# Expert steps of 1024 inner columns instead of 512

## The chip, the cores and the metric

The kernel runs on one core of a Trainium2 chip. The metric is the device time of one execution in microseconds (us). Before the change it was 2018.52 us, the median of three runs (2017.03, 2019.66 and 2018.52).

A core has a matrix engine (PE, with its weight loads listed apart as PEld), a vector engine (DVE), a scalar engine (ACT), a general engine (POOL) and an engine that here only issues DMAs (SP). Each runs its own instruction stream in order; semaphores join them. PE writes into eight banks of PSUM (each 128 x 512 float32), and ACT and DVE read them from there into SBUF.

## The reference

The reference is a backbone of two layers over 256 latent tokens with a context prefix of 256 tokens, 1024 wide: a mixer of three kinds of attention heads and then a feed-forward block, each with a norm, a modulation and a gated residual. The feed-forward block of the first layer is dense. That of the second takes about half of the time, and the change touches it alone: a router picks two of eight experts for each latent token, and each expert is a SwiGLU with 3584 inner columns.

```python
def swiglu(h, w_gate, w_up, w_down):
    return (jax.nn.silu(h @ w_gate) * (h @ w_up)) @ w_down

def moe_swiglu(h, w_router, w_gate, w_up, w_down):
    logits = (h @ w_router).astype(jnp.float32)
    top_v, top_i = lax.top_k(logits, TOP_K)          # 2 of 8
    top_w = jax.nn.softmax(top_v, axis=-1)
    combine = ...                                    # weight of each expert for each token, mostly 0
    out = jnp.zeros_like(h)
    for e in range(N_EXPERTS):                       # w_gate[e], w_up[e]: 1024 x 3584, w_down[e]: 3584 x 1024
        out = out + combine[..., e:e + 1] * swiglu(h, w_gate[e], w_up[e], w_down[e])
    return out
```

Everything is float32. The three matrices of an expert are 14 MB each, 336 MB for the eight, and all of it is read.

## The kernel before

**Arithmetic.** A product of float32 matrices is done as three PE matmuls on parts: each operand is split exactly into a high and a low part (w = h + l, both of a type that PE multiplies fast), and h·h, l·h and h·l are added up in one PSUM bank (`mm3`, lines 289 to 291). A weight arrives by DMA as a raw tile of 1 MB. Each piece of half a tile (128 x 1024 elements) is then split: ACT casts the high part (line 150), DVE subtracts it from the raw tile for the low part (line 151). Both write one buffer `whl`, of which there are four, so the split runs up to four pieces ahead of PE. The helper `split` (lines 295 and 296) does the same for activations: a cast on ACT, then a subtraction on DVE.

**The ring of raw tiles.** SP issues the loads in the order of use (line 138) into a ring of 8 + `NRAWM` = 13 raw tiles; a load waits until DVE has subtracted the tile that was in its buffer.

**An expert.** The tokens of an expert sit in 128 slots, as two transposed parts `xh` and `xl`. The 3584 inner columns are worked through in 7 steps of 512. A step s has these parts, in the order in which the main loop (lines 1644 to 1672) emits them:

- `turn(s)`: PE transposes the activations of step s by four 128 x 128 transposes into one bank `pt` (line 1518), ACT copies `gh` from it (line 295), DVE subtracts `gl` (line 296).
- `gate_up(s + 1)` for the gate and then for up: 8 chunks of rows, 3 matmuls of 512 columns each, into one bank `pg` and one bank `pu` (lines 1496 and following, matmuls on lines 289 to 291).
- `activate(s + 1)`: ACT takes the silu of `pg`, DVE multiplies by `pu`, into a buffer `sg` (lines 1510 and 1511).
- `down(s)`: 4 chunks of the 512 inner columns by the two halves of the 1024 output columns, 24 matmuls that add into two banks `pd`, which are held through all steps of an expert.

So PE turns the results of a step only after the down products of the step before it, and there is always the gate and up of one step between a turn and the down products that use it.

**The small work between the matmuls.** After every piece of weights the function `tick` counts, and at every third tick it emits one closure from a queue: the result of the expert before (`weigh`, `high` and `low`: `yt` on DVE, line 1566, `yh` on ACT, line 1569, `yl` on DVE, line 1572), its scatter back to the tokens (a pair of matmuls into a bank `psc`, lines 1580 and 1581, and an addition to `xl` on DVE, line 1585), the gathering of the tokens for the next pair of experts (8 matmuls into a bank `pgt`, line 1468, `gtmp` on ACT or DVE, then a split into `xh` and `xl`) and the transposed one-hot rows (bank `pw`). What hasn't been emitted in time is emitted by `flush` ahead of the next expert's gate products or ahead of the first down products.

**Buffers.** Banks of PSUM come from two groups of four. Group b holds `pg` and `pu`. Group c holds the two `pd`, and everything else (`pt`, `pgt`, `psc`, `pw`) shares its other two. Buffers go round in order of request, and a new use of a buffer waits until the last reader of the old one is done. `sg`, `gh`, `gl`, `yt`, `yh`, `yl` and `gtmp` share `NT2M` = 6 SBUF buffers of 128 x 512 in the same way.

**Order.** In this stage PE, ACT and DVE keep the order in which the program is written: an instruction that waits holds up all that is behind it on its engine.

Of the kernel before, what the change touches and what calls it, by code (L numbers as in the profile page):

```python
# [29 lines left out]
NSTEP = DFE // 512  # L30
GRID_W = 64

# columns of the table of constants
# [10 lines left out]
NRAWM, NSPLITM, NT2M, NXG = 5, 4, 6, 2  # L44
# [3 lines left out]
BR = 4  # L48
# [20 lines left out]
def _constants():  # L69
    """Identity, triangles, selectors and the rotary tables: they depend on the shapes alone."""  # L70
# [35 lines left out]
def reverse(t):  # L106
    """[p, n] read from the last column to the first."""
    (ps, p), (_, n) = t.ap
    return bass.AP(tensor=t.tensor, offset=t.offset + n - 1, ap=[[ps, p], [-1, n]])
# [6 lines left out]
class Weights:  # L116
    """The weights in the order in which they are used: loads run ahead in a ring, and each float32 tile is
    split exactly into two float32r parts (w = h + l), in one or two pieces, shortly before its products."""
# [54 lines left out]
    def take(self, key, j=0):  # L173
        """The next piece: its two parts, or itself where it isn't split; as [128, nk, n]."""
        i, p, _, _ = self.pieces[self.ntake]
        assert self.plan[i][0] == key and p == j, (self.plan[i][0], p, key, j)
        self.pump()
        self.ntake += 1
        return self.hl[self.ntake - 1] if self.plan[i][2] else self.raw[i]
# [12 lines left out]
def rows_of(w, r0, nk, c0, n):  # L192
    """nk chunks of 128 rows from r0, columns c0..c0+n, as [128, nk, n]."""
    return w[r0:r0 + nk * 128, c0:c0 + n].rearrange("(k p) f -> p k f", p=128)
# [40 lines left out]
def down_tiles(s):  # L235
    """Tiles of the weights of a step: first chunk of 128 rows, chunks, first column, columns. In the last step one half of
    the columns after the other, so that most of what follows goes on beside it."""
    if s < NE * NSTEP - 1:
        return [(0, 2, 0, D), (2, 2, 0, D)]
    return [(r, 2, c, 512) for c in (0, 512) for r in (0, 2)]  # L240


def moe_plan(I):
    plan = []

    def gu(m, s):
        e, n = divmod(s, NSTEP)
        for h in range(2):
            plan.append(((m, s, h), rows_of(I[m][0, e], 512 * h, 4, 512 * n, 512), True))

    S = NE * NSTEP
    for s in range(S + 1):
# [3 lines left out]
        if s > 0:  # L256
            e, n = divmod(s - 1, NSTEP)
            for h, (r, nk, c, cols) in enumerate(down_tiles(s - 1)):
                plan.append((("moe_down", s - 1, h), rows_of(I["moe_down"][0, e], 512 * n + 128 * r, nk, c, cols), True))
# [8 lines left out]
# the blocks of 512 columns of the modulations in the order in which they are worked out  # L268
# [8 lines left out]
def kernel(ctx: ExitStack, tc: tile.TileContext, I, out: bass.AP):  # L277
# [15 lines left out]
    def split(h, l, x):  # L293
        """h + l = x, both float32r."""
# [106 lines left out]
    # silu of the two conditions, the norms' weights and the biases of the modulations, as columns  # L401
# [21 lines left out]
    def mod_block(l, n):  # L423
        """512 columns of the modulation of both streams."""
# [39 lines left out]
    def gate_rows(l, which, streams, new=lambda: t2("grow")):  # L464
        """The gate of the residual, the same in every row: per stream two tiles of 512 columns."""
# [12 lines left out]
    def rstd(b):  # L478
        """1 / rms of the tokens of a block."""
# [12 lines left out]
    def norm_T(l, which, steps, hT):  # L492
        """Into hT, by steps of (stream, chunks of 128 columns in pairs). The product with diag(1 / rms) turns and scales a block."""
# [34 lines left out]
    def ordered(engines):  # L528
        """A region in which these engines keep to the program's order."""
        return tc.manual_schedule(engines={getattr(mybir.EngineType, e) for e in engines})  # L530

    def drain(gen):
        """Run a generator to its end; its value."""
# [10 lines left out]
    def merge(one, two):  # L544
        """Steps of both in turn to the end of `one`; its value."""
# [16 lines left out]
    def alternate(one, two, n):  # L562
        """n steps of `one`, a step of `two`, and so on to the end of both."""
# [11 lines left out]
    def weave(main, fill, every=1):  # L575
        """Emit both, one step of `fill` after every `every` steps of `main`; their values."""
# [18 lines left out]
    def take_in(l, name, hT, step):  # L595
        """The products of a projection by its tiles of weights: step(k, tile's parts, flags)."""
# [10 lines left out]
    def proj_T(l, name, hT, outs):  # L607
        """Columns in the partitions: outs of (bank, its rows, first column, tokens)."""
# [7 lines left out]
    def proj_nat(l, name, hT, nb=4, late=False, group="c"):  # L616
        """Tokens in the partitions, 256 columns: two blocks of 128 tokens in a bank."""
# [8 lines left out]
        if late:  # L626
            # the context first: the latent tokens are ready after it
# [16 lines left out]
    def inputs_gla(l, hT, A):  # L644
# [17 lines left out]
        for r in range(2):  # L662
            # 2 silu(z) = (tanh(z / 2) + 1) z: tanh lies in one table with exp
# [5 lines left out]
    def gla(l, A, mix):  # L669
# [4 lines left out]
        # sums of the log decays (times 16) along each chunk, forward or backward  # L674
# [10 lines left out]
        for d in range(2):  # L685
# [31 lines left out]
            # the states: what each chunk adds, then the walk over the chunks  # L717
# [52 lines left out]
    def head_norm(po, n):  # L770
        """1 / rms over the 64 rows of each head, spread over these rows: po two of [2 heads x 64, n]; [128, n] each."""
# [22 lines left out]
    # rotary tables with the norms' weights and the scale of the scores  # L794
# [30 lines left out]
    def rotate(dst, src, nh, d, cos, sin):  # L825
        """dst = src * cos + swapped halves of src * sin: [128, 2 blocks, nh heads * d], the tables per block."""
# [15 lines left out]
    def head_rstd(src, nh):  # L842
        """1 / rms of nh heads of 64 in two blocks."""
# [10 lines left out]
    def gqa_heads(l, b2, j, src, nh):  # L854
        """Norm and rotary of nh heads of 64 in two blocks (j: 0 q, 1 k)."""
# [12 lines left out]
    def diff_maps(b2, src, scale, t):  # L868
        """Rotary of the 8 maps of 32 in two blocks, times scale."""
# [10 lines left out]
    def stack(t3, kind):  # L880
        """The parts h and l of heads [128, n, d] side by side, for products that contract over 128 rows and hold
        every product of parts: per head h|l (q of GQA), h|h l|l (its k), h|h|l|l (q of a map), h|l|h|l (their k)."""
# [9 lines left out]
    def turned(o, dst):  # L892
        """Transposed into dst [128, 4, 128 tokens]."""
# [7 lines left out]
    def evac(dst, src):  # L901
        """A bank to SBUF, by turns on two engines."""
# [3 lines left out]
    def inputs_diff(l, hT, A, norm):  # L906
        """The operands of the differential heads; in the first layer by the first half of the columns of x while the
        modulations of the others arrive."""
# [56 lines left out]
    def inputs_gqa(l, hT, A):  # L965
        """Keys and values of GQA, then its queries: the four heads of a key head."""
# [27 lines left out]
    def attention(l, A, mix, fill, rate):  # L994
        """Units of four score tiles each (a block of queries, and four maps or heads), as a pipeline: the queries of a
        unit, the scores of the one before and the products with V of the one before that; `fill` between them."""
# [5 lines left out]
        def place(u, g):  # L1002
            """Tile and columns of a score tile: with 256 keys two of them share a tile."""
# [40 lines left out]
        def weigh(u):  # L1044
            """Exponentials into weights: of GQA times 1 / sum, of the two maps their difference."""
# [89 lines left out]
        def at(j, f):  # L1135
            """f of the unit j, as steps."""
# [45 lines left out]
    def products(order, parts, weights, step, nb, end):  # L1182
        """All blocks of tokens by each chunk in turn; by the last two block after block, so that the first are done early."""
# [18 lines left out]
    def order_of(nb):  # L1202
        """Blocks of tokens, the context first."""
        return (2, 3, 0, 1) if nb == 4 else (0, 1)

    def advance(norm, b):
        """Steps of the next norm of the context before the residuals of the latent tokens."""
# [50 lines left out]
    def early():  # L1258
        """The first weights of the experts, as soon as those of the modulations have been used."""
# [33 lines left out]
    def ffn(norm, hT, norm2):  # L1293
        drain(alternate(norm, mods(MODS["ffn"]), EVN[0]))
        act = []
        for j in range(6):
# [6 lines left out]
            for m in ("ffn_gate", "ffn_up"):  # L1303
# [3 lines left out]
                if m == "ffn_gate" and j == 0:  # L1307
                    # the context first: the latent tokens are ready after it
# [73 lines left out]
    def spread(b):  # L1382
        """x / rms in two parts."""
# [5 lines left out]
    # the two largest logits, the lower expert first where they are equal, and their softmax  # L1389
# [7 lines left out]
    # the gate of the residual, while the logits are compared  # L1397
# [12 lines left out]
    # slot of a token with an expert, from 1: how many tokens up to it have chosen it; 0 where it hasn't  # L1410
# [9 lines left out]
    def rest_of_route():  # L1420
        """What isn't needed for the first products: the weights of the experts and the largest number of their tokens."""
# [14 lines left out]
    def experts(W, off):  # L1436
        """Slots off..off+128 of every expert."""
# [18 lines left out]
        def gather(p, d2):  # L1456
            """Columns 256 * d2 .. of the tokens of experts 2p and 2p + 1, modulated, as steps: the products, the parts of
            the first, and later those of the second."""
# [37 lines left out]
        def gate_up(s, m, store):  # L1496
            e = s // NSTEP
            p = store[s] = bank("p" + m[4], "b")
            h_, l_ = XG[e]
            for q in range(4):  # L1500
                wh, wl = W.take((m, s, q // 2), q % 2)
                for kk in range(2):
                    k = 2 * q + kk
                    mm3(p, (h_[:, k], l_[:, k]), (wh[:, kk], wl[:, kk]), start=k == 0, stop=k == KC - 1)
# [3 lines left out]
        def activate(s):  # L1508
            g = t2("sg")
            S.activation(g, ps_g.pop(s), AF.Silu)  # L1510
            V.tensor_tensor(g, g, ps_u.pop(s), op=ALU.mult)
            act[s] = g
# [225 lines left out]
```

## Time and profile before

| what | before |
|---|---|
| median of three runs | 2018.52 us |
| profiled execution: its span, the only time that the page gives for it | 2016.9 us |
| PE busy | 1930.0 us (96%) |
| DVE busy | 1408.0 us (70%) |
| ACT busy | 1182.3 us (59%) |
| read from memory | 469.53 MB |

The page takes one execution on the chip: busy time per engine, the span in 40 slices, the transfers, and the costliest groups of instructions by line. Matmuls are pipelined, so the durations of neighbouring ones overlap and the distance between two starts is what one costs PE. PEclk is the clock that PE was granted: 1.00 is 2.4 GHz, and about half of that is the lower level of 1.2 GHz. The experts' stage is the stretch from about 980 us to about 2000 us; it has little in common with the stages ahead of it, so the argument uses stretches inside it rather than the shares of the page.

### The profile page before, as it was taken

How to read it: one execution, taken by the hardware profiler on the slowest of the kernel's cores; microseconds unless marked ns; L12 is line 12 of the kernel's file. 1: busy time of each engine (PE TensorE's matmuls, PEld its weight loads, DVE VectorE, ACT ScalarE, POOL GpSimd, SP SyncE). 2: the span in 40 equal slices, each digit the busy share in tenths (PEclk: the TensorE clock that was granted, in tenths of full speed). 3: DMA queues.
4: the chain of work that ended last, by engine and by line, in shares of the span. 5: the costliest groups of instructions: out<-in, count | busy, mean ns of one | idle time of the engine just before them, and what ended most of it. 6: DMA issues, size and time to landing. Idle time of an engine off the chain costs nothing. (4 is left out here: it accounts for less than half of the span.)

```text
span 2016.9 us, 26581 instructions
## 1 busy us (share of the span) xinstructions
PE 1930.0 (96%) x10205; PEld 1544.9 (77%) x10205; DVE 1408.0 (70%) x1844; ACT 1182.3 (59%) x1623; POOL 63.3 (3%) x79
## 2 busy tenths in 40 slices
PE   6998989999999999989999999999999999999997
PEld 3875857788887879767788788787887878878785
DVE  2456674522324246576899888998888988889897
ACT  3445463522224226544677778777787777877775
POOL 2001210000000000120000000000000000000000
PEclk9999989999999999989899999999999999999998
DMA  8754123433334233242699999999999999999990
GB/s 274 275 187 161 45 77 105 136 101 119 94 97 154 94 126 127 75 165 107 252 369 364 330 341 346 338 371 329 347 338 333 366 334 349 339 338 361 332 340 32
DMA packets 215239, 472.40 MB, mean 234 GB/s; under 512 B 8860, under 2 KB 29648, under 8 KB 215104
## 3 DMA queue, kind: packets, MB, share of 16 engines
q1 hardware_dynamic: 213712, 469.35, 66.3%
q8 instruction: 82, 1.34, 0.3%
q0 software_dynamic: 608, 0.35, 0.2%
q10 hardware_dynamic: 784, 0.93, 0.1%
q14 instruction: 53, 0.43, 0.1%
HBM read 469.53 MB, written 1.05 MB: 233 GB/s over the span
## 5 line engine op out<-in xcount | busy, mean ns | idle before, releaser
L151 DVE TENSOR_TENSOR whl<-raw,whl 128x1024 fp32r<-128x1024 f32 (+1 forms) x676 | 809.2, 1216 | 84.3 <-ACT whl L150 79.1
L150 ACT CAST whl<-raw 128x1024 fp32r<-128x1024 f32 (+1 forms) x676 | 702.3, 1046 | 202.6 <-PE pu L291 74.3
L151 DVE TENSOR_TENSOR whl<-wraw,whl 128x1024 fp32r<-128x1024 f32 (+1 forms) x122 | 145.6, 1193 | 290.3 <-ACT whl L150 290.3
L150 ACT CAST whl<-wraw 128x1024 fp32r<-128x1024 f32 (+1 forms) x122 | 125.3, 1027 | 327.5 <-PE pf L291 166.2
L289 PE MATMUL pg<-whl,xh 128*128 128x512 f32 x448 | 183.6, 410 | 7.3 <-ACT whl L150 6.9
L290 PE MATMUL pg<-whl,xh 128*128 128x512 f32 x448 | 180.2, 402 | 5.4 <-DVE whl L151 5.4
L291 PE MATMUL pg<-whl,xl 128*128 128x512 f32 x448 | 179.7, 401 | 0.2
L289 PE MATMUL pu<-whl,xh 128*128 128x512 f32 x448 | 177.8, 397 | 0.0
L290 PE MATMUL pu<-whl,xh 128*128 128x512 f32 x448 | 176.9, 395 | 0.0
L289 PE MATMUL pd<-whl,gh 128*128 128x512 f32 x448 | 176.9, 395 | 0.0
L291 PE MATMUL pu<-whl,xl 128*128 128x512 f32 x448 | 176.9, 395 | 0.0
L291 PE MATMUL pd<-whl,gl 128*128 128x512 f32 x448 | 176.8, 395 | 0.0
L290 PE MATMUL pd<-whl,gh 128*128 128x512 f32 x448 | 176.6, 394 | 0.0
L289 PE MATMUL pf<-hh,whl 128*128 128x512 f32 (+1 forms) x368 | 139.3, 380 | 0.7 <-ACT mg L436 0.7
L290 PE MATMUL pf<-hl,whl 128*128 128x512 f32 (+1 forms) x368 | 139.7, 380 | 0.0
L291 PE MATMUL pf<-hh,whl 128*128 128x512 f32 (+1 forms) x368 | 139.6, 380 | 0.0
L289 PE MATMUL pn<-whl,hh 128*128 128x256 f32 x400 | 117.1, 293 | 0.9 <-ACT hh L522 0.9
L291 PE MATMUL pn<-whl,hl 128*128 128x256 f32 x400 | 114.3, 286 | 0.9 <-DVE hl L524 0.9
L290 PE MATMUL pn<-whl,hh 128*128 128x256 f32 x400 | 113.5, 284 | 0.0
L289 PEld LDWEIGHTS pg<-whl,xh 128*128 128x128 f32 x448 | 86.0, 192 | 27.1 <-ACT whl L150 8.6
L290 PEld LDWEIGHTS pg<-whl,xh 128*128 128x128 f32 x448 | 85.9, 192 | 25.6 <-DVE whl L151 7.7
L291 PEld LDWEIGHTS pg<-whl,xl 128*128 128x128 f32 x448 | 85.8, 191 | 21.5 <-DVE xl L296 1.8
(328 smaller groups left out, 3231.9 us busy)
## 6 DMA issues: line engine op xcount, KB each, us to landing
raw<-in_moe_gate_dram SPq DMA_DIRECT2D x112, 1024.0 KB, 6.0
raw<-in_moe_up_dram SPq DMA_DIRECT2D x112, 1024.0 KB, 5.9
raw<-in_moe_down_dram SPq DMA_DIRECT2D x110, 1024.0 KB, 5.8
wm<-in_w_mod_dram SPq DMA_DIRECT2D x48, 1024.0 KB, 6.4
wraw<-in_w_in_dram SPq DMA_DIRECT2D x32, 512.0 KB, 3.7
wraw<-in_ffn_gate_dram SPq DMA_DIRECT2D x22, 512.0 KB, 3.5
wraw<-in_ffn_up_dram SPq DMA_DIRECT2D x22, 512.0 KB, 3.5
wraw<-in_ffn_down_dram SPq DMA_DIRECT2D x22, 512.0 KB, 3.2
```

The lines of the kernel that those rows point to most:

```text
L150: self.keep(self.nc.scalar.copy(h, t))
L151: self.keep(self.nc.vector.tensor_tensor(l, t, f32(h), op=ALU.subtract))
L289: PE.matmul(o, lh, rh, start=start, stop=False, **kw)
L290: PE.matmul(o, lh, rl, start=False, stop=False, **kw)
L291: PE.matmul(o, ll, rh, start=False, stop=stop, **kw)
```

## The change

The inner columns of an expert are worked through in three steps of 1024 and one of 512 instead of seven of 512. What follows from it:

- A raw tile of gate or up weights holds 2 chunks of 128 rows with 1024 columns (rows of 4 KB in memory) instead of 4 chunks with 512 columns (rows of 2 KB). It is 1 MB either way, and the number of tiles, pieces and matmuls is the same.
- In a wide step `gate_up` adds into two banks `pg` and two `pu`, three matmuls to the one and three to the other in turn; these four are all of group b.
- `activate` makes two `sg`, and `turn` makes twice: four transposes into a bank `pt`, `gh`, `gl`.
- `down` takes 8 chunks (4 tiles).
- `NRAWM` goes from 5 to 4 (12 raw tiles in the ring), `NT2M` from 6 to 10, and `BR`, the step at which the one-hot rows are turned, from 4 to 2, as an expert has four steps now.

Some comments and empty lines also differ, which moves line numbers: 150 and 151 become 152 and 153, 289 to 291 become 292 to 294, 295 and 296 become 298 and 299, the transposes of `turn` move from 1518 to 1527, `yt`, `yh` and `yl` to 1577, 1580 and 1583, the pair into `psc` to 1591 and 1592, the addition to 1596, the gather's matmuls to 1471.

```diff
-NSTEP = DFE // 512
+WIDTHS = (1024, 1024, 1024, 512)
+NSTEP = len(WIDTHS)
+STEPS = [(e, sum(WIDTHS[:n]), w) for e in range(NE) for n, w in enumerate(WIDTHS)]
...
-NRAWM, NSPLITM, NT2M, NXG = 5, 4, 6, 2
+NRAWM, NSPLITM, NT2M, NXG = 4, 4, 10, 2
...
-BR = 4
+BR = 2
...
-        return [(0, 2, 0, D), (2, 2, 0, D)]
+        return [(r, 2, 0, D) for r in range(0, STEPS[s][2] // 128, 2)]
...
-        e, n = divmod(s, NSTEP)
-        for h in range(2):
-            plan.append(((m, s, h), rows_of(I[m][0, e], 512 * h, 4, 512 * n, 512), True))
+        e, c, w = STEPS[s]
+        nk = 2048 // w
+        for h in range(KC // nk):
+            plan.append(((m, s, h), rows_of(I[m][0, e], 128 * nk * h, nk, c, w), True))
...
         def gate_up(s, m, store):
-            e = s // NSTEP
-            p = store[s] = bank("p" + m[4], "b")
+            e, _, w = STEPS[s]
+            p = store[s] = [bank("p" + m[4], "b") for _ in range(w // 512)]
             h_, l_ = XG[e]
-            for q in range(4):
+            nk = 1024 // w
+            for q in range(KC // nk):
                 wh, wl = W.take((m, s, q // 2), q % 2)
-                for kk in range(2):
-                    k = 2 * q + kk
-                    mm3(p, (h_[:, k], l_[:, k]), (wh[:, kk], wl[:, kk]), start=k == 0, stop=k == KC - 1)
+                for kk in range(nk):
+                    k = nk * q + kk
+                    for i, pi in enumerate(p):
+                        f = slice(512 * i, 512 * i + 512)
+                        mm3(pi, (h_[:, k], l_[:, k]), (wh[:, kk, f], wl[:, kk, f]), start=k == 0, stop=k == KC - 1)
                 W.done(s < NS - 1 or m != "moe_up" or q < 2)
                 tick()
...
         def turn(s):
-            pt = bank("pt", "c")
-            g = act[s]
-            for c in range(4):
-                PE.transpose(pt[:, 128 * c:128 * c + 128], g[:, 128 * c:128 * c + 128], ident)
-            h, lo = t2("gh", F32R), t2("gl", F32R)
-            split(h, lo, pt)
-            act[s] = (h, lo)
+            for i, g in enumerate(act[s]):
+                pt = bank("pt", "c")
+                for c in range(4):
+                    PE.transpose(pt[:, 128 * c:128 * c + 128], g[:, 128 * c:128 * c + 128], ident)
+                h, lo = t2("gh", F32R), t2("gl", F32R)
+                split(h, lo, pt)
+                act[s][i] = (h, lo)
```

`activate` and `down` are changed to match.

How the instructions move is seen in three places. In the rows, `whl` is the split weight piece, and the names in brackets are the engines (or DMA rings) whose semaphores an instruction waits for.

The first place is ACT at the border between the first two experts. Before, the second `yh` (the second half of the first expert's result) stands just ahead of the casts for the next expert's gate products and waits for DVE and for PE: its buffer is that of a `gh` that the last down products read.

```order
L150 CAST whl<-raw 128x1024 [waits DVE_49,PE_49]
L1510 ACTIVATE sg<-pg 128x512
L1569 CAST yh<-yt 128x512 [waits DVE_49,PE_49]
L150 CAST whl<-raw 128x1024 [waits DMAHW7_49,Activation_49]
L150 CAST whl<-raw 128x1024 [waits Activation_49]
L150 CAST whl<-raw 128x1024 [waits DMAHW0_49,Activation_49]
L150 CAST whl<-raw 128x1024 [waits PE_49,Activation_49]
L295 CAST gh<-pt 128x512 [waits PE_49]
```

After the change it has a buffer that is free, and waits for DVE alone.

```order
L152 CAST whl<-raw 128x1024 [waits DMAHW4_49,DVE_49,PE_49]
L152 CAST whl<-raw 128x1024 [waits DVE_49,PE_49]
L152 CAST whl<-raw 128x1024 [waits DMAHW5_49,DVE_49,PE_49]
L1580 CAST yh<-yt 128x512 [waits DVE_49]
L152 CAST whl<-raw 128x1024 [waits PE_49,Activation_49]
L152 CAST whl<-raw 128x1024 [waits DMAHW6_49,DVE_49,PE_49]
L152 CAST whl<-raw 128x1024 [waits DVE_49,PE_49]
L1519 ACTIVATE sg<-pg 128x512
```

What moved: the wait for PE on line 1569 is gone on line 1580, and the casts behind it no longer stand behind a PE wait.

The second place is PE at a turn of the second expert, between the down products and the next gate products. Before:

```order
L289 MATMUL pd<-whl,gh 128x512
L290 MATMUL pd<-whl,gh 128x512
L291 MATMUL pd<-whl,gl 128x512
L1518 MATMUL pt<-cst,sg 128x128 [waits DVE_49,PE_49]
L1518 MATMUL pt<-cst,sg 128x128 x3
L289 MATMUL pg<-whl,xh 128x512 [waits Activation_49]
L290 MATMUL pg<-whl,xh 128x512 [waits DVE_49]
```

After (the third turn of the second expert):

```order
L292 MATMUL pd<-whl,gh 128x512
L293 MATMUL pd<-whl,gh 128x512
L294 MATMUL pd<-whl,gl 128x512
L1527 MATMUL pt<-cst,sg 128x128 x4
L1527 MATMUL pt<-cst,sg 128x128 [waits DVE_49]
L1527 MATMUL pt<-cst,sg 128x128 x3
L292 MATMUL pg<-whl,xh 128x512 [waits Activation_49]
L293 MATMUL pg<-whl,xh 128x512
L294 MATMUL pg<-whl,xl 128x512
```

What moved: there are eight transposes instead of four, and the fifth waits for DVE. Its bank is the one that the first four transposes filled (the other one of group c still holds gathered tokens), and the value it waits for is that of the `gl` which empties it.

The third place is DVE at the first down products of the third expert, where the second half of the second expert's result is split. Before:

```order
L1511 TENSOR_TENSOR sg<-sg,pu 128x512 [waits Activation_49]
L1566 SCALAR_TENSOR_TENSOR yt<-pd,ws,mg 128x512 [waits DVE_49]
L1572 TENSOR_TENSOR yl<-yt,yh 128x512 [waits PE_49,Activation_49]
L151 TENSOR_TENSOR whl<-raw,whl 128x1024 [waits DMAHW7_49,Activation_49]
```

After:

```order
L153 TENSOR_TENSOR whl<-raw,whl 128x1024 [waits DMAHW0_49,Activation_49]
L1577 SCALAR_TENSOR_TENSOR yt<-pd,ws,mg 128x512
L153 TENSOR_TENSOR whl<-raw,whl 128x1024 [waits Activation_49]
L1520 TENSOR_TENSOR sg<-sg,pu 128x512 [waits Activation_49] x2
L1583 TENSOR_TENSOR yl<-yt,yh 128x512 [waits PE_49,Activation_49]
L153 TENSOR_TENSOR whl<-raw,whl 128x1024 [waits DMAHW1_49,Activation_49]
```

What moved: this `yl` still waits for PE, but for a matmul in the middle of the down products of the new expert's first step (the 11th that adds into the second `pd`), with the subtraction for those products' third piece behind it.

## Rows read from the trace of the kernel before

In rows of windows the columns are the stretch, its length, then for each engine busy time and number of instructions, PEclk, the busy share of the DMA engines and GB/s. In rows of a timeline they are start, length, engine, line, operation, output and inputs, number, and in brackets the idle time ahead with what ended it. In grouped lines, the busy time, the mean length in ns and the idle time ahead follow the bar.

**Rows 1.** The page, first part: the span and each engine's busy time.
```profile
span 2016.9 us, 26581 instructions
PE 1930.0 (96%) x10205; PEld 1544.9 (77%) x10205; DVE 1408.0 (70%) x1844; ACT 1182.3 (59%) x1623; POOL 63.3 (3%) x79
```

**Rows 2.** Windows of 50 us inside the experts' stage.
```profile
1300.00:1350.00 50.00, 50.00 (x226) 40.70 (x226) 45.54 (x42) 38.92 (x41) 0.00 (x0) 1.00 1.02 366
1500.00:1550.00 50.00, 48.25 (x207) 38.67 (x206) 45.45 (x48) 36.10 (x40) 0.00 (x0) 0.97 0.95 342
```

**Rows 3.** Waits from 960 to 1960 us: total, times, longest, in us.
```profile
ACT yh L1569 <- PE pd L290: 29.9, 7, 4.3
...
PE pg L289 <- ACT whl L150: 6.9, 7, 1.0
...
PE pg L290 <- DVE whl L151: 5.4, 7, 0.8
```

**Rows 4.** Waits of SP's DMA queue from 960 to 1960 us.
```profile
SPq L138 <- DVE whl L151: 829.5, 311, 14.0
```

**Rows 5.** Timeline of ACT at the first border between experts.
```profile
1134.76 0.62 ACT L1569 CAST yh<-yt 128x512 fp32r<-128x512 f32 x1 [4.27 <-PE pd L290]
```

**Rows 6.** Timeline of PE at the same border.
```profile
1134.79 0.60 PE L1518 MATMUL pt<-cst,sg 128*128 128x128 f32 x4
1136.38 0.49 PE L289 MATMUL pg<-whl,xh 128*128 128x512 f32 x1 [0.98 <-ACT whl L150]
1137.64 0.51 PE L290 MATMUL pg<-whl,xh 128*128 128x512 f32 x1 [0.77 <-DVE whl L151]
...
1138.44 0.61 PE L290 MATMUL pg<-whl,xh 128*128 128x512 f32 x1
...
1141.83 0.41 PE L289 MATMUL pg<-whl,xh 128*128 128x512 f32 x1
```

**Rows 7.** Windows of the lower clock, first and last of four.
```profile
1138.44:1141.83 3.39, 3.39 (x9) 2.65 (x8) 3.39 (x5) 2.16 (x3) 0.00 (x0) 0.50 0.54 161
...
1780.20:1783.60 3.40, 3.40 (x9) 2.63 (x10) 3.40 (x4) 2.90 (x4) 0.00 (x0) 0.51 0.39 92
```

**Rows 8.** Timeline of PE at a turn inside an expert.
```profile
1030.31 0.39 PE L291 MATMUL pd<-whl,gl 128*128 128x512 f32 x1
1030.54 0.60 PE L1518 MATMUL pt<-cst,sg 128*128 128x128 f32 x4
1030.90 0.48 PE L289 MATMUL pg<-whl,xh 128*128 128x512 f32 x1
1031.21 0.39 PE L290 MATMUL pg<-whl,xh 128*128 128x512 f32 x1
```

**Rows 9.** Timeline of ACT at the same turn.
```profile
1031.70 0.58 ACT L295 CAST gh<-pt 128x512 fp32r<-128x512 f32 x1
```
**Rows 10.** Timeline of DVE at the same turn.
```profile
1031.83 1.23 DVE L151 TENSOR_TENSOR whl<-raw,whl 128x1024 fp32r<-128x1024 f32 x1 [0.17 <-ACT whl L150]
1032.97 0.68 DVE L296 TENSOR_TENSOR gl<-pt,gh 128x512 fp32r<-128x512 f32 x1
```

**Rows 11.** Lines grouped by form, 1000 to 1950 us.
```profile
L151 DVE TENSOR_TENSOR whl<-raw,whl 128x1024 fp32r<-128x1024 f32 x628 | 755.5, 1223 | 77.6 <-ACT whl L150 72.7
...
L291 PE MATMUL pd<-whl,gl 128*128 128x512 f32 x416 | 164.2, 395 | 0.0
...
L1572 DVE TENSOR_TENSOR yl<-yt,yh 128x512 fp32r<-128x512 f32 x14 | 9.6, 689 | 17.9 <-PE pt L1518 17.9
```

**Rows 12.** Timeline of PE at a gather, first and last of 8 matmuls.
```profile
1189.68 0.28 PE L1468 MATMUL pgt<-oh,xnh 128*128 128x256 f32 x1
...
1190.51 0.28 PE L1468 MATMUL pgt<-oh,xnl 128*128 128x256 f32 x1
```

**Rows 13.** DMA issues, 1000 to 1950 us: count, KB each, median us to landing.
```profile
raw<-in_moe_down_dram SPq DMA_DIRECT2D x104, 1024.0 KB, 5.9
raw<-in_moe_gate_dram SPq DMA_DIRECT2D x104, 1024.0 KB, 5.8
```

More of the change, by code (lines that the diff above doesn't have):

```diff
@@ L256, in moe_plan @@
         if s > 0:
-            e, n = divmod(s - 1, NSTEP)
+            e, f, _ = STEPS[s - 1]
             for h, (r, nk, c, cols) in enumerate(down_tiles(s - 1)):
-                plan.append((("moe_down", s - 1, h), rows_of(I["moe_down"][0, e], 512 * n + 128 * r, nk, c, cols), True))
+                plan.append((("moe_down", s - 1, h), rows_of(I["moe_down"][0, e], f + 128 * r, nk, c, cols), True))
     return plan
@@ L1508, in activate @@
         def activate(s):
[L1509 to L1512, printed above, removed]
-        def turn(s):
-            pt = bank("pt", "c")
-            g = act[s]
-            for c in range(4):
-                PE.transpose(pt[:, 128 * c:128 * c + 128], g[:, 128 * c:128 * c + 128], ident)
-            h, lo = t2("gh", F32R), t2("gl", F32R)
-            split(h, lo, pt)
-            act[s] = (h, lo)
+            act[s] = []
+            for pg, pu in zip(ps_g.pop(s), ps_u.pop(s)):
+                g = t2("sg")
+                S.activation(g, pg, AF.Silu)
+                V.tensor_tensor(g, g, pu, op=ALU.mult)
+                act[s].append(g)
+        def turn(s):
+            for i, g in enumerate(act[s]):
[5 more added lines that the diff above has]
+                act[s][i] = (h, lo)
         def down(s):
@@ L1526, in down @@
                 PD[e] = [bank("pd", "c") for _ in range(2)]
-            h_, l_ = act.pop(s)
+            last = STEPS[s][2] // 128 - 1
             for i, (r, nk, c, cols) in enumerate(down_tiles(s)):
@@ L1530, in down @@
                     wh, wl = W.take(("moe_down", s, i), j)
-                    k = slice(128 * (r + j), 128 * (r + j) + 128)
+                    h_, l_ = act[s][(r + j) // 4]
+                    k = slice(128 * ((r + j) % 4), 128 * ((r + j) % 4) + 128)
                     for f in range(0, cols, 512):
                         mm3(PD[e][(c + f) // 512], (h_[:, k], l_[:, k]), (wh[:, 0, f:f + 512], wl[:, 0, f:f + 512]),
-                            start=n == 0 and r + j == 0, stop=n == NSTEP - 1 and r + j == 3)
+                            start=n == 0 and r + j == 0, stop=n == NSTEP - 1 and r + j == last)
                     W.done()
@@ L1541, in down @@
                         f()
+            act.pop(s)
         def before_result(e):
```

## The prediction

> **What bounds the kernel now.** The page comes first, for the scale only: PE is busy for 96% of a span of 2016.9 us, DVE for 70%, ACT for 59% [rows 1]. Those are means over stages, so I look next at 50 us windows of the stage that the change touches. There PE is busy for 50.00 of 50.00 us at the full clock, DVE for 45.54, ACT for 38.92; the window that holds a border between experts is the exception: PE 48.25 at a mean clock of 0.97 [rows 2]. So the stage is bound by PE, with DVE not far behind, and the number of matmuls is the same before and after. What the change can move is the time in which PE stands or is slowed.
>
> The view of waits says where it stands. PE waits for no transfer. It waits 7 times for a cast (6.9 us) and 7 times for a subtraction (5.4 us) ahead of the gate products, and ACT waits 7 times with `yh` for down products, 29.9 us in all [rows 3]. There are 7 borders between experts. SP's queue waits 829.5 of 1000 us for a free raw tile [rows 4]: the loads are paced by PE, not the other way round.
>
> The timeline of the first border shows the mechanism. `yh` stands for 4.27 us until the last down products have let go of its buffer [rows 5]; the casts behind it are late, and PE's first gate product starts 1.59 us after the transposes, its second 1.26 us after the first [rows 6]. At a turn without trouble these distances are 0.36 and 0.31 us [rows 8]. So a border costs 1.23 + 0.95 = 2.18 us, and the clock then falls to half for 3.39 us [rows 7]. In that stretch eight matmuls start 3.39 us apart [rows 6]; at 0.23 us each [rows 8] they would take 1.84, so a fall costs 1.55 us. There are four such stretches in the stage, after four of the seven borders.
>
> **What the change removes.** With ten buffers instead of six, `yh` at the border waits for no PE instruction, so the casts run ahead as elsewhere. Gone: 7 x 2.18 = 15.3 us, and the falls of the clock behind them, 4 x 1.55 = 6.2 us. Sum: 21.5 us. What is late next there is the gate's first piece, four pieces ahead of PE as at any turn: nothing.
>
> **What it adds.** `turn` now wants two banks of group c at once. Two of the four are held by the `pd`, so it gets two only if no gather, scatter or one-hot product holds one. Where one is held, the second four transposes need the bank of the first four, and PE, in program order, stands until `gl` has emptied it. The price is in the trace: from the first transpose at 1030.54 [rows 8], `gh` starts at 1031.70 [rows 9], `gl` behind a weight subtraction at 1032.97 and ends at 1033.65 [rows 10]: 3.11 us, and some 0.07 until PE sees it. Four transposes take 0.36 to 0.44, so PE stands for 3.11 + 0.07 - 0.44 = 2.74 us. Before, this latency was hidden by a whole step of gate and up products; now those products stand behind the waiting transposes. By places, following each semaphore value to its instruction (experts counted from 0):
>
> - B: third turn of experts 1, 3 and 5 (a gather's bank is held): 2.74, and 2.9 with the one-hot comparison on DVE near it in one of them. 3 x 2.9 = 8.7.
> - E: turn after the first step of experts 2, 4 and 6 (a scatter's bank is held). The addition of that scatter and a weight subtraction stand ahead of `gl`, for which I add a third of such a subtraction (1.22 us [rows 11]): 3.1. 3 x 3.1 = 9.3.
> - C: last turn of experts 1, 3 and 5, where the last two gathers are flushed. The second gather needs the bank of the transposes; the first gather's eight matmuls (1190.51 - 1189.68 plus one more distance of 0.12: 0.95 us [rows 12]) cover part: 3.18 - 0.44 - 0.95 = 1.8, and 2.2 with the activations of the first gather on ACT and DVE in between. 3 x 2.2 = 6.6.
> - D: first down products of experts 2, 4 and 6. `yl` waits for the 11th matmul into the second `pd`, whose end I put 0.43 after its start; then `yl` (0.69 [rows 11], its successor 0.60 after its start), then a subtraction (1.22 [rows 11]) for the second matmul of the next piece, which PE wants three starts or 0.70 after that 11th one. 0.43 + 0.60 + 1.22 + 0.07 - 0.70 = 1.6. 3 x 1.6 = 4.8.
> - A: turn after the first step of experts 1, 3, 5 and 7. The banks are free, but a scatter six matmuls later wants the first one: 3.18 - 0.44 - 0.44 - 6 x 0.23 = 0.9; with up to 0.4 for the second transposes, which wait for the addition of the scatter before, 1.3. 4 x 1.3 = 5.2.
>
> Sum of the standing: 34.6 us. The turns that meet free banks cost nothing by themselves: two `gl` stand in a row on DVE, but PE has four pieces split ahead, and the number of subtractions is unchanged.
>
> The clock is the second part of the price. Before, a border's standing of 0.98 and 0.77 us was followed by a fall in four of seven cases [rows 6, 7]. B, C, D and E are 12 stretches of standing of that size or longer. At the same rate of 4 in 7 there are 7 falls, 7 x 1.55 = 10.9 us; the ends are none and 12, 0 and 18.6 us.
>
> "Perfetto Trace Analysis" of the Trainium skill, section "Matmuls", asks that independent groups of matmuls rotate through different PSUM banks, so that emptying one overlaps the next. By that rule the change takes from group c just the bank that did so; rows 8 to 10 agree in that the four transposes are followed at once by products into another bank, and the price by those rows is the 2.74 us above.
>
> **Loads.** Gate and up rows are 4 KB instead of 2 KB, and the ring holds 12 tiles instead of 13. Tiles of down weights have rows of 4 KB already, and land 5.9 us after issue, those of the gate with 2 KB rows 5.8 [rows 13]. So nothing is won in the row length, and a ring that SP waits for 829.5 us [rows 4] doesn't miss one tile: with three times 104 tiles in 950 us [rows 13], one per 3 us, twelve are about 36 us of lead over a landing of 5.9. I cost both at nothing; the cover is SP's waiting, and without it a tile less would be 3 us once.
>
> **Sum.** 2016.9 - 21.5 + 34.6 + 10.9 = 2040.9 us as a profiled span. The span of before is 1.6 below the median of its runs, so 2042.5, rounded to 2042 us.
>
> **Bounds.** From below: `gl` without the subtraction ahead of it in half of the places takes half of 1.22 off the mean, so B, E 2.4 each, C 1.6, D 1.4, A 0.7: 14.4 + 4.8 + 4.2 + 2.8 = 26.2, with 3 falls (4.7): 2016.9 - 21.5 + 26.2 + 4.7 + 1.6 = 2027.9. From above: one more subtraction ahead of half of the `gl`, so B and E 3.6, C 2.8, D 2.0, A 2.0: 21.6 + 8.4 + 6.0 + 8.0 = 44.0, with 12 falls: 2016.9 - 21.5 + 44.0 + 18.6 + 1.6 = 2059.6.
>
> **The rivals.**
>
> 1. Faster: the borders are freed, and the new waits don't reach PE. It speaks for it that 1996 to 1997 is simply 2016.9 - 21.5 + 1.6, and that nothing but standing time is at stake. Its place is the second transposes, its condition that the other bank has been emptied when they are due, or `gl` ends within 0.44 us of the first; rows 8 to 10 say 3.11 us, seven times that. To come out faster at all, the standing and falls together must stay under 21.5: not even the lower bound of the standing alone does. For it is only that I may have put a bank's release too late. Time 1997; chance 0.05.
> 2. Faster by the loads: if transfers set the pace, PE's new standing would only take the place of waiting for them, and longer rows would shorten that. The DMA engines are busy for 0.95 to 1.02 of the windows [rows 2], which speaks for it; that PE waits for none of them and SP for PE [rows 3, 4], and that rows of 4 KB land no earlier [rows 13], speaks against. The time would lie between the 1997 of a PE that never stands and the 2018.5 of before, say 2008; chance 0.02. The Trainium skill, "Perfetto Trace Analysis", section "DMA Optimizations", says that going from transfers of 2 KB to larger ones can improve throughput much when a kernel is bound by DMA; by rows 4 that condition isn't met here.
> 3. No change: the standing is at its lower bound (26.2) and the clock hardly falls: 2016.9 - 21.5 + 26.2 + 1.6 = 2023, a hair over the line. With one place less it is within it. Chance 0.08.
> 4. Much slower: DVE falls behind at the double turns. It is busy for nine tenths [rows 2]; a turn makes it wait for ACT, and after it the subtractions for the next gate pieces may be late, as at the border of before (0.77 us [rows 6]). At 20 of the 24 double turns that is 20 x 0.77 = 15 us more: 2058, and with a fall of the clock behind a few of them 2065. Chance 0.14.
>
> The forecast itself has 0.71.
>
> **Chances.** What can be told from no change here is about 0.2% (4 us), so slower means above 2022.6. Slower: 0.71 + 0.14 and a little of the third, 0.87. Within: the rest of the third, 0.06. Faster: the first two, 0.07. The range holds 8 in 10 from the lower bound, taken down to 2025 for the third rival, to the upper bound at 2059.
>
> **What would show it.** Right: in the waits of after, `yh` behind PE is gone from the list, and PE has `pt` waiting for `gl`, 6 times about 2.7 to 3.3 us, `pgt` waiting for `gl` 3 times about 2, `psc` for `gl` 4 times about 1, and a gate or down product waiting for a subtraction behind `yl` 3 times about 1.6. The border windows show no gap in experts 0, 2, 4 and 6. The stretches at half clock number more than four, and each lies right behind one of these gaps. DMA landing stays near 5.9 us or SP's waiting near 800 us. Wrong: if those gaps are there but PE stands also for `whl` at ordinary turns, the fourth rival; if `pt` waits for `gl` under 1 us, I have mistaken the latency, and the time goes towards the first; if PE waits for raw tiles, the ring was too small after all.

## The result and the profile after

The changed kernel takes 2038.13 us (median of four runs, 2036.16 to 2041.52) against 2018.22 us of before (four runs): the ratio is 1.0098, with a 95% interval from 1.0086 to 1.0110. It is slower by 17 to 22 us, as forecast; 2042 us was predicted, with a range of 2025 to 2059.

The page after, first part, answers to [rows 1]: the busy times are those of before within 5 us, the span is 22.8 us longer.

```profile
span 2039.7 us, 26567 instructions
PE 1934.2 (95%) x10205; PEld 1549.5 (76%) x10205; DVE 1409.4 (69%) x1844; ACT 1187.1 (58%) x1623; POOL 63.2 (3%) x79
```

Of these 22.8 us, 3.9 lie ahead of the experts, where the two programs are the same: the first gate product starts at 984.3 us before and at 988.2 after by the timelines of PE. A second profile of the changed kernel starts it at 982.8, so this is a difference between executions. Another 1.3 us lie behind the last scatter. All that follows is therefore measured from the start of the first gate product to the start of the last scatter matmul: 1019.3 us before, 1036.8 after. The stage is 17.5 us longer.

The view of waits from 960 to 2000 us, after (total, times, longest), answers to [rows 3].

```profile
PE pt L1527 <- DVE gl L299: 15.6, 6, 2.6
ACT gh L298 <- PE pt L1527: 14.8, 6, 2.7
...
DVE yl L1583 <- PE pd L293: 6.0, 3, 2.0
...
PE pgt L1471 <- DVE gl L299: 5.9, 3, 2.0
...
PE pd L293 <- DVE whl L153: 4.6, 3, 1.5
...
PE psc L1591 <- DVE gl L299: 3.3, 4, 0.8
```

The `yh` that waited for PE, and the gate products behind it, are gone from the list. In their place stand PE's own waits: `pt` for `gl` six times (B and E), `pgt` for `gl` three times (C), a down product for a subtraction behind `yl` three times (D), `psc` for `gl` four times (A). No line of PE names a raw tile.

At place B, PE's timeline reads as follows (the third turn of the second expert; at the ordinary turn of [rows 8] the first gate product starts 0.36 us behind the first transpose).

```profile
1205.14 0.60 PE L1527 MATMUL pt<-cst,sg 128*128 128x128 f32 x4
1208.30 0.66 PE L1527 MATMUL pt<-cst,sg 128*128 128x128 f32 x4 [2.56 <-DVE gl L299]
1208.71 0.48 PE L292 MATMUL pg<-whl,xh 128*128 128x512 f32 x1
```

And ACT's and DVE's, which answer to [rows 9] and [rows 10].

```profile
1206.29 0.58 ACT L298 CAST gh<-pt 128x512 fp32r<-128x512 f32 x1
...
1206.42 1.22 DVE L153 TENSOR_TENSOR whl<-raw,whl 128x1024 fp32r<-128x1024 f32 x1 [0.16 <-ACT whl L152]
1207.56 0.68 DVE L299 TENSOR_TENSOR gl<-pt,gh 128x512 fp32r<-128x512 f32 x1
```

From the first transpose to the end of `gl` it is 1208.24 - 1205.14 = 3.10 us, as before (3.11). The latency hasn't changed; now PE waits it out.

Place E and place A on PE: at E the second four transposes wait, at A the scatter.

```profile
1302.23 0.60 PE L1527 MATMUL pt<-cst,sg 128*128 128x128 f32 x4
1305.46 0.66 PE L1527 MATMUL pt<-cst,sg 128*128 128x128 f32 x4 [2.64 <-DVE gl L299]
...
1169.27 0.40 PE L294 MATMUL pg<-whl,xl 128*128 128x512 f32 x1
1170.49 0.50 PE L1591 MATMUL psc<-yh,oT 128*128 128x512 f32 x1 [0.82 <-DVE gl L299]
```

Place C on PE, where the first gather behind the last turn of an expert ends and the second waits, then place D on PE:

```profile
1233.98 0.28 PE L1471 MATMUL pgt<-oh,xnl 128*128 128x256 f32 x1
1236.23 0.39 PE L1471 MATMUL pgt<-oh,xnh 128*128 128x256 f32 x1 [1.96 <-DVE gl L299]
...
1294.40 0.40 PE L292 MATMUL pd<-whl,gh 128*128 128x512 f32 x1
1296.32 0.50 PE L293 MATMUL pd<-whl,gh 128*128 128x512 f32 x1 [1.52 <-DVE whl L153]
```

And place D on DVE:

```profile
1294.44 0.69 DVE L1583 TENSOR_TENSOR yl<-yt,yh 128x512 fp32r<-128x512 f32 x1 [1.99 <-PE pd L293]
1295.05 3.49 DVE L153 TENSOR_TENSOR whl<-raw,whl 128x1024 fp32r<-128x1024 f32 x3
```

The distance of 1.92 us between the two down products, less the usual 0.23, is D's price: 1.69. At D, DVE had been idle for 1.99 us with work queued behind `yl`.

The clock, in the windows of the half level, after (columns as in [rows 7]): there are four again.

```profile
1306.00:1309.80 3.80, 3.80 (x12) 2.99 (x11) 0.79 (x2) 1.63 (x2) 0.00 (x0) 0.55 1.02 374
1469.96:1473.37 3.41, 2.94 (x9) 2.55 (x10) 1.11 (x2) 0.59 (x1) 0.00 (x0) 0.50 1.01 383
1500.80:1504.30 3.50, 3.50 (x10) 2.77 (x10) 0.43 (x1) 2.21 (x4) 0.00 (x0) 0.53 0.77 293
1831.70:1835.20 3.50, 3.50 (x10) 2.72 (x9) 0.82 (x2) 1.59 (x2) 0.00 (x0) 0.51 0.98 346
```

They lie behind the first E (PE resumes at 1305.46), at the second B, behind the second C and behind the third E. At the second B the clock is at the half level from 1469.96 us, while PE still stands (it resumes at 1470.43); at the other three it falls after PE has resumed. The price of a fall is the time of PE's next 34 starts behind the gap, less that of the same starts at a like place without a fall: 9.02 - 7.47 = 1.55 at the first E, 7.94 - 6.62 = 1.32 at the second B, 8.65 - 7.10 = 1.55 at the second C, 9.04 - 7.47 = 1.57 at the third E. Together that is 6.0 us.

The loads, answering to [rows 13]: rows of 4 KB land no earlier than rows of 2 KB did.

```profile
raw<-in_moe_down_dram SPq DMA_DIRECT2D x103, 1024.0 KB, 5.8
raw<-in_moe_gate_dram SPq DMA_DIRECT2D x102, 1024.0 KB, 6.1
```

### The profile page after: what moved, and what is told of

Its sections match the earlier page's. It is cut to its first block, busy times and chain, and to the rows that moved or that the text cites. A ratio compares the mean times of both kernels' runs of the same rounds, so it can differ in the third digit from the quotient of the medians.

```text
span 2039.7 us, 26567 instructions
## 1 busy us (share of the span) xinstructions
PE 1934.2 (95%) x10205; PEld 1549.5 (76%) x10205; DVE 1409.4 (69%) x1844; ACT 1187.1 (58%) x1623; POOL 63.2 (3%) x79
## 2 busy tenths in 40 slices
DMA packets 166087, 472.40 MB, mean 232 GB/s; under 512 B 8860, under 2 KB 29648, under 8 KB 165952
## 5 line engine op out<-in xcount | busy, mean ns | idle before, releaser
L293 PEld LDWEIGHTS pd<-whl,gh 128*128 128x128 f32 x448 | 84.3, 188 | 25.5 <-DVE whl L153 5.9
L292 PEld LDWEIGHTS pg<-whl,xh 128*128 128x128 f32 x448 | 85.8, 192 | 19.6 <-ACT xh L298 0.7
```

The source lines that it names most:

```text
L292: PE.matmul(o, lh, rh, start=start, stop=False, **kw)
L293: PE.matmul(o, lh, rl, start=False, stop=False, **kw)
```

## The experiments

The theory is that of the prediction: the time is the standing of PE at the named places and the falls of the clock behind some of them. The rivals are that a wide step is slower by itself, and that something other than the number of shared buffers freed the borders.

**The kernel before with ten buffers.**

```diff
-NRAWM, NSPLITM, NT2M, NXG = 5, 4, 6, 2
+NRAWM, NSPLITM, NT2M, NXG = 4, 4, 10, 2
```

> The kernel before with ten shared buffers instead of six (and 12 raw tiles instead of 13), steps of 512 kept. The prediction's own words make the ten buffers the reason why the border waits go: then 7 x 2.18 us of standing and four falls of the clock go, 21.5 us, and the time is about 1997 us. Rival: in the built program yh at the border still sits on a buffer that a gh of the running down products holds, as released buffers are taken again before unused ones; then yh still waits for PE 7 times, about 4.3 us at the longest, and the time stays at 2018 us within 4 us. The rival is held likelier.

Measured: 2001.58 us, ratio to before 0.9903 (0.9873 to 0.9932). The rival that I held likelier fell; its assignment of buffers was misread. ACT's timeline at the first border shows that `yh` waits for `yt` alone, for 2.39 us instead of 4.27 [rows 5].

```profile
1131.50 0.62 ACT L1569 CAST yh<-yt 128x512 fp32r<-128x512 f32 x1 [2.39 <-DVE yt L1566]
1132.03 3.89 ACT L150 CAST whl<-raw 128x1024 fp32r<-128x1024 f32 x4
```

PE there, to be compared with [rows 6]:

```profile
1133.41 0.60 PE L1518 MATMUL pt<-cst,sg 128*128 128x128 f32 x4
1133.77 0.47 PE L289 MATMUL pg<-whl,xh 128*128 128x512 f32 x1
1134.39 0.50 PE L290 MATMUL pg<-whl,xh 128*128 128x512 f32 x1
```

The first gate product starts 0.36 us behind the transposes, the second 0.62 behind the first instead of 0.31. Of 2.18 us per border 0.3 to 0.4 are left, and no window of the stage is at the half clock. The stage takes 999.2 us, 20.0 less than before, where 21.5 was predicted for the whole. So the prediction's gain was real, it came from the buffers, and it doesn't need wider steps. The raw ring has one tile less here, as in the changed kernel.

**The kernel before with result buffers of their own.**

```diff
-            t, h, lo = t2("yt"), t2("yh", F32R), t2("yl", F32R)
+            t, h, lo = (mo.tile([128, 512], dt, name=nm, tag="ty", bufs=5)
+                        for nm, dt in (("yt", F32), ("yh", F32R), ("yl", F32R)))
```

The raw ring is 11 tiles here.

> The kernel before with five buffers of their own for yt, yh and yl (and 11 raw tiles instead of 13), steps of 512 kept. If the border waits cost what the prediction says (7 x 2.18 us and the falls behind them, 21.5 us), the time is 1995 to 1999 us, with no wait of yh for PE and no fall of the clock inside the stage. Rival: the standing is only moved (PE stands there for the next late cast, or DVE falls behind), then more than 2008 us. If a ring of 11 tiles were too small, PE would wait for raw tiles, which it has not done so far.

Measured: 1999.50 us, half a microsecond above the expected range; ratio 0.9891 (0.9862 to 0.9920), stage 1000.1 us, no fall of the clock inside it. `yh` waits 2.4 us for `yt` as in the experiment before, and no line of PE names a raw tile. Two ways to free the buffer give the same stage within 0.9 us, which confirms that it was the buffer.

**The changed kernel, transposes in group b.**

```diff
-                pt = bank("pt", "c")
+                pt = bank("pt", "b")
```

> The changed kernel with the bank of the transposes taken from group b, which is free at that time, instead of group c. If the second transposes, the gather and the scatter stand for a bank of group c (places A, B, C and E), 28.4 us of standing go, and those falls of the clock that follow them (at most four, 6 us); what is left is the subtraction behind yl three times, 5.4 us. Time 2003 to 2010 us. Rival: wide steps are slower by themselves (two gl in a row on DVE, longer landing of rows of 4 KB): then PE stands for whl instead, and the time stays above 2025 us.

Measured: 2005.24 us, ratio to before 0.9916 (0.9887 to 0.9945); stage 1005.8 us, 30.9 less than the changed kernel. One word takes the kernel from 1.0% slower to 0.8% faster. In the waits of PE the places A, B, C and E are gone; D stands as it was, and one wait is new.

```profile
PE pd L293 <- DVE whl L153: 4.6, 3, 1.5
...
PE pu L292 <- DVE gl L299: 2.1, 1, 2.1
```

The new one is at the first turn of all, on PE: it is emitted after the first gate products have taken two banks of group b, so that the up products want the bank of the transposes at once.

```profile
1018.93 1.04 PE L1527 MATMUL pt<-cst,sg 128*128 128x128 f32 x8
1022.09 0.50 PE L292 MATMUL pu<-whl,xh 128*128 128x512 f32 x1 [2.12 <-DVE gl L299]
```

Behind it the clock falls once (1.6 us). The rival that wide steps are slower by themselves would have left the time above 2025 us; it fell.

**The same, with result buffers of their own.** The two edits above in the changed kernel, with five result buffers, eight shared ones and 11 raw tiles.

> The changed kernel with the bank of the transposes from group b, and five buffers of their own for yt, yh and yl beside eight shared ones (11 raw tiles instead of 12). Then no wait of those named is left, neither for a bank nor behind yl: 1996 to 2001 us, no fall of the clock inside the stage. It differs from the kernel before with own result buffers by the step width alone: with rows of 4 KB and 1024 columns worth nothing the two are within 4 us of each other; if longer rows help or wide steps hurt by themselves, the difference shows it.

Measured: 2001.00 us, ratio 0.9898 (0.9869 to 0.9926), stage 1000.1 us. D is gone: 5.7 us less than the stage of the run before, against 3 x 1.69 + 3 x 0.1 that D and the slower start behind it took. So D hung on a shared buffer too: with ten of them `yl` still got one that the running down products were reading. The expectation said that no wait of those named is left, but overlooked the one of the first turn, 2.3 us and a fall of 1.6.

**The best of the wide kernels.**

```diff
-                pt = bank("pt", "b")
+                pt = bank("pt", "b" if s else "c")
```

> The changed kernel with own result buffers and the transposes' bank from group b, as in the run before, but for the very first turn, which takes it from group c again (it is made after the first gate products have taken two banks of group b, so that there the up products stood for it, 2.4 us and a fall of the clock of 1.6 us behind). Expected: 4 us less than that run, about 1997 us, with no standing of PE above 0.4 us between the start of the experts and the last down products. Rival: the fall of the clock comes elsewhere, then some 2 us less only.

Measured: 1998.38 us, ratio 0.9890 (0.9874 to 0.9907). The stage takes 996.0 us, 4.1 less than the run before, as expected. The profiled execution as a whole gains nothing over that run's (2000.25 against 1999.63 us), because it began the experts at 988.8 us instead of 984.2; for the executions without a profile, on which the medians rest, this is not shown. In the windows PE is busy throughout at the full clock, and DVE as much as in [rows 2].

```profile
1150.00:1200.00 50.00, 50.00 (x220) 40.56 (x220) 46.33 (x46) 38.68 (x41) 0.00 (x0) 1.00 0.97 354
1300.00:1350.00 50.00, 50.00 (x224) 40.66 (x223) 45.40 (x44) 38.37 (x41) 0.00 (x0) 1.00 0.99 358
```

This is faster than both kernels. Against the narrow steps with result buffers of their own (1000.1 us) the stage is 4.1 us shorter; there, seven borders have a second gate product 0.3 us late with a start 0.1 us late behind it, and three gathers hold a gate product up by 0.2 with 0.1 behind it, together 3.9 us. So what the wide steps saved is nearly all that, and longer rows in themselves show nothing. The intervals of this version and of the two with narrow steps (1999.5 and 2001.6 us) overlap.

**Both kernels profiled again.**

> The changed kernel unaltered, profiled a second time, to see what of its time is the same in two executions. The standing belongs to the program: the same places and sizes within 0.1 us, 33 to 34 us in all. The falls of the clock need not: 4 in the first profile, 7 by the prediction's rate; if gaps of this size bring a fall at a fixed rate of 4 in 12, 2 to 6 here, and after other gaps than in the first profile. The 4 us that the first profile had more ahead of the experts is expected to be gone, as that part of the program is the same in both kernels.

Measured: 2036.11 us, stage 1036.9 us against 1036.8. The standing is the same at all 16 places within 0.05 us, 33.0 us in all; the experts begin at 982.8 us. The four stretches of half clock are there too, 6.0 us in all, and against my expectation at the very same gaps as in the first profile: first E, second B, second C, third E.

```profile
1300.50:1304.10 3.60, 3.60 (x11) 2.77 (x11) 0.71 (x2) 1.63 (x2) 0.00 (x0) 0.53 1.04 393
1464.55:1467.96 3.41, 3.02 (x9) 2.57 (x10) 1.03 (x2) 0.58 (x1) 0.00 (x0) 0.50 1.02 393
1495.30:1498.80 3.50, 3.50 (x11) 2.74 (x10) 0.42 (x1) 2.12 (x4) 0.00 (x0) 0.52 0.78 308
1826.20:1829.70 3.50, 3.50 (x11) 2.71 (x10) 0.72 (x2) 1.63 (x2) 0.00 (x0) 0.52 1.05 394
```

> The kernel before unaltered, profiled a second time, for the same reason: 7 borders with 2.2 us of standing each, and 2 to 6 falls of the clock (4 in the first profile), each right behind a border.

Measured: 2018.09 us, stage 1019.4 us, the seven borders at 2.18 us each and four falls, 6.2 us. They lie behind the first, third, fifth and sixth border; in the first profile it was the first, third, fourth and sixth.

## Why the prediction was right, point by point

It was right in direction, in place and in size, and 4 us too high. The terms, with what the runs measured:

| term | predicted, us | measured, us |
|---|---|---|
| standing at the borders, gone | 7 x 2.18 = 15.3 | 7 x 2.18 in both profiles of before, none of it after |
| falls of the clock behind them, gone | 6.2 | 6.2 in both profiles of before |
| B | 3 x 2.9 = 8.7 | 3 x 2.72 = 8.2 |
| E | 3 x 3.1 = 9.3 | 2.80 + 2.78 + 2.80 = 8.4 |
| C | 3 x 2.2 = 6.6 | 3 x 2.12 = 6.4 |
| D | 3 x 1.6 = 4.8 | 3 x 1.69 = 5.1 |
| A | 4 x 1.3 = 5.2 | 4 x 0.99 and 4 x 0.25 = 5.0 |
| falls of the clock after | 10.9 | 6.0 in both profiles of after |
| sum | +24.0 | +17.6 by these terms, +17.5 by the stage |

The measured standing is a distance between starts of matmuls less the usual distance of that kind (0.232 us, 0.11 for transposes, 0.12 in a gather); the falls are measured as in the section on the result. Starts 0.06 to 0.2 us late, which are not in the table, stand in both kernels, some 1.7 us before (at the seven borders and three gathers) and 1.8 after (behind A to E and at the gathers), and so nearly cancel.

**What held.** That PE bounds the stage and waits for no load; that the border waits hang on a shared buffer (the first two experiments); that a turn wants two banks where often one is free, and that PE then waits out the latency of `gh` and `gl` (the third experiment, which takes 30.9 us off the stage by moving that bank). SP's wait for a free raw tile is 834.0 us after, beside [rows 4], and neither PE nor ACT waits for a raw tile, so the ring of 12 was no shortage either. Eleven tiles came nearer to one: in the second and the fourth experiment ACT's casts waited for raw tiles 41 and 67 times, 15.5 and 25.5 us in all, though PE still did not. No gate or up product waits for `whl` after, so the fourth rival, DVE falling behind at the double turns, had no case. Of the two rules of the Trainium skill ("Perfetto Trace Analysis", sections "Matmuls" and "DMA Optimizations"), that on rotating PSUM banks agreed with the trace (six waits of 2.7 to 2.8 us where there was none to rotate to); that on longer transfers had no case here, since PE waits for none. The addition of a third of a subtraction at E was unnecessary: the nearest row, unaltered, gave 2.74 us, and 2.80 was measured.

**What was mis-sized.** The step "at the same rate of 4 in 7 there are 7 falls" failed: there were 4 at 12 gaps, 6.0 us instead of 10.9. That is 4.9 of the 6.5 us by which the stage is shorter than predicted; the standing makes 1.5 more (33.1 us instead of 34.6). The price of one fall was right (1.55 us predicted, 1.3 to 1.6 measured). That the stretches would number more than four was wrong with it; that each lies right behind one of these gaps was right but for the second B, where the clock fell while PE still stood. Counting by gaps with one rate doesn't fit these runs: behind D there was none in nine cases (two profiles of the changed kernel and the third experiment), at E four in six, at B and C two in six each, and both profiles of the changed kernel have them at the same gaps.

**What was only lucky.** The 2038.13 us lie 4 us below the forecast, but the stage was forecast 6.5 us too long. The medians differ by 19.9 us and the profiled stages by 17.5; what is more lies outside the stage, for which the prediction had no term. Ahead of the experts the changed kernel took 3.9 us more than before in the first pair of profiles and 0.6 us less in the second, so that part varies between executions. Behind the last scatter it took 1.3 and 1.2 us more; what makes these is not shown.

## What to carry to other kernels

When a step is made larger, count what it wants at once from each pool of banks and buffers, and who holds the rest at that moment; here the price of one bank too few was the whole latency of the operations that empty it (2.72 us), and PE, which keeps program order in this stage, paid it in full. A gain and a loss that come in one change can be had apart: here the buffers alone took about 1.0% off (the first experiment), the width with its transposes in group c put about 1.8% on, and the bank's group, one word, decided the sign.

## What the runs showed of the hardware

The half clock came back at the same four of 12 gaps in two executions of the changed kernel, though PE stands equally long (2.72 us) at the first, second and third B and only the second brings it, before PE has resumed; in two executions of before it was behind the first, third and sixth border both times and once behind the fourth, once behind the fifth. So neither the length of a gap alone nor chance alone decides. What does was not settled by these runs.

Rows of 4 KB against 2 KB lowered the number of packets on the page from 215239 to 166087 for the same 472.40 MB, and the landing time of a 1 MB tile of the gate went from 5.8 to 6.1 us.
